# Key tiles summed in float32 while the activations are made, in a two-block transformer kernel

## The chip, the cores and the metric

One Trainium2 chip, one of its cores. The metric is device time in microseconds for one execution of the whole program, as the median of several runs; smaller is better.

## What is computed

Two transformer blocks on 256 tokens of width 2048, in float32. The part that matters is the passage from the first layer to the second: the layer norm of layer 0 ends, its result is scaled and shifted by the modulation of the condition vector, and keys, values and a forget gate are projected from it.

```python
def shared_kv(x, c_act, w_mod_kv, b_mod_kv, w_kv, b_f):
    mod = c_act @ w_mod_kv + b_mod_kv
    shift, scale = jnp.split(mod, 2, axis=-1)
    hk = x * (1.0 + scale[:, None]) + shift[:, None]
    kvf = hk @ w_kv
    k, v, zf = jnp.split(kvf, [B_WIDTH, 2 * B_WIDTH], axis=-1)
    ...
```

Here `hk` is 256 x 2048 and `w_kv` is 2048 x 4112: 16 column tiles of 128 for the keys, as many for the values, and 16 columns for the gate. Ahead of it stands layer 0 (differential attention, output projection, layer norm), behind it forgetting attention with its query/gate projection and output projection, then a second block: a state-space mixer (S5) with a gated output (GLU) and an MLP.

## The kernel before

Activations lie transposed: 16 tiles (index kt, or j where they are made) of 128 channels by 256 tokens.

**Projections.** A float32 product is made of three matmuls on reduced-precision float32 (fp32r): the weights are split into a high part `wh` and a remainder `wl`, the activations likewise into `aH` and `aL`. `mm_t` (L153) sums one column tile: for each of 16 kt, `wh` with `aH` (L163), `wh` with `aL` (L164), `wl` with `aH` (L165), 48 matmuls. `mm_n` (L188) does the same for the values with activations and weights exchanged. The weights of one column tile are 1 MB, loaded as two halves on SP's queue into four `raw` buffers and split by ScalarE (`wh`, L134) and VectorE (`wl`, L135) into five buffers of each kind. `prefetch` (L140) does this two column tiles ahead.

**Background work.** `weights()` (L144) is called once for each column tile. Apart from the prefetch it issues one step of background work (`bg`, L293) and one or more steps of a side job (`step`, L273). The background work is the modulation sums, matrix-vector products in 224 steps over the whole program, named m0, mk, m1, mc, m12, m2 and so on: each step loads two blocks of 512 KB (`graw`, four buffers, L268) and adds them up on TensorE (L222) or on VectorE into `gacc` (L237), as a cyclic list for each stage says ("policy"; the sums of mc run on TensorE always). Eight steps make a half, which TensorE closes (L246, L252). The order of the jobs is fixed, so a step not issued in one stage is issued in the next. A step's sum is issued one call behind its load. `bg_finish` issues what is left of a job where its result is needed.

**Side jobs.** In the key/value stage the side job is `s5_outputs_table` (L599), a generator that is resumed 33 times and makes a table for the later S5 mixer in 16 blocks: VectorE products (`vprod`, L554 and L555) and their sums (L635, L637), ScalarE copies (L644 to L646), small matmuls `kps` (L649) and stores. In the query/gate stage and the output projection of layer 1 it is `ctx_states` (L1279), which starts when mc is closed and is resumed 42 times: an opening with `sf` (L1296), then eight blocks of five steps each, with matmuls `inc` (L697) and on VectorE a tree of products and sums (L1337 to L1340) that ends in a copy (L1343). What is left of a side job at the end of its stage is issued by `flush`.

**Order.** The program is written in one order and a scheduler, which simulates the engines, puts the instructions of each engine's queue in the order in which they run; what is earlier in the program has priority among what is ready. `issue_after(x)` puts the instructions of its block that are on x's engine behind x; those on other engines are not bound.

**The passage.** `layer1` (L1118) makes the activations `k_` in `affine_split` (L412): for each j, `norm` adds and multiplies on VectorE (L1112, L1113), ScalarE makes `u` (L417) and its high part (L419), VectorE the remainder `kL` (L420). Six background steps follow (`BG_K`, L1126). Then come 16 key tiles by `mm_t` and 16 calls of `mm_n` for the values, the gate's sums `zf` (L1143 to L1145) behind the first key tile, and ScalarE copies of the results (L1183, L1192), each followed for the keys by a scaling of the residual in place (L1184). Next stages: the affine of the second normed input, query/gate tiles, output projection with norm, S5.

**A similar piece further on.** The GLU opens the sums of four column pairs while its own activations are still being made, in float32 with unsplit weights (`open_sums`, L1453 to L1461), in the same PSUM pool `pj` (four banks) that the projections use.

The small tiles `u` come from a pool of six buffers that other short-lived tiles share.

Of the kernel before, what the change touches and what calls it, by code (L numbers as in the profile page):

```python
# [3 lines left out]

# [7 lines left out]
F32 = mybir.dt.float32  # L12
F32R = mybir.dt.float32r
I32 = mybir.dt.int32
AF = mybir.ActivationFunctionType
# [6 lines left out]
T = 256  # L22
KT = 16
# [23 lines left out]

KO_J = 4
KO_K = 8
P_START = ("pe",)  # L50
P_L0A = ('dve', 'pe')
P_KV = ('dve', 'pe')
# [15 lines left out]
BG_K = 6  # L68
# [13 lines left out]
E_K = "x"  # L82
# [24 lines left out]
class K:  # L107
# [164 lines left out]

    def step(self):  # L273

        while self.side and next(self.side[0], True):
            self.side.pop(0)

    def flush(self, job):
        while job in self.side:
# [422 lines left out]
    def run(self):  # L702
        tc, I = self.tc, self.I
        from contextlib import ExitStack
        with ExitStack() as es:
            pool = lambda name, bufs, **kw: es.enter_context(tc.tile_pool(name=name, bufs=bufs, **kw))
            dp = pool("scratch", 1, space=DRAM)
            self.d_w = dp.tile([16, 128, 1024], F32, name="d_w")
            self.d_v = dp.tile([8, 128, 16, 128], F32, name="d_v")
            self.d_m = dp.tile([16, 128, 256], F32, name="d_m")  # L710
            self.d_l = dp.tile([128, 16, 128], F32, name="d_l")
            self.d_pw = dp.tile([128, 6, 512], F32, name="d_pw")
            self.d_b = dp.tile([16, 128, 256], F32, name="d_b")
            self.cp = pool("consts", 1)
            self.vt = pool("vecs", 1)
            self.sm = pool("small", 6)
            self.raw = pool("raw", 4)
            self.rg = pool("rg", 4)
            self.t1 = pool("t1", 6)
            self.ga = pool("ga", 1)  # L720
            self.sq = pool("sq", 2)
            self.pj = pool("pj", NPJ, space=PSUM)
            self.m = pool("m", 8 - NPJ, space=PSUM)
            xr = pool("xres", 1)
            self.hl = pool("hl", HL)
            self.bgq = []
            self.late = []
            self.hold = HOLD
            self.steps = itertools.cycle((1,))
            self.open = False  # L730
            self.side = []
            self.x = xr.tile([128, KT, T], F32, name="xres")
            mod = lambda n: self.vt.tile([128, KT], F32, name=n)
            self.m0 = [mod(f"m0_{i}") for i in range(3)]
            self.m1 = [mod(f"m1_{i}") for i in range(3)]
            self.mk = [mod(f"mk_{i}") for i in range(2)]
            self.m2 = [mod(f"m2_{i}") for i in range(6)]
            self.mc = [mod(f"mc_{i}") for i in range(2)]
            w0, w1, wk, w2 = I["w_mod0"], I["w_mod1"], I["w_kvmod"], I["w_mod2"]
            g0 = lambda i: (f"m0_{i}", self.gemv(w0, 6144, i, "c", [self.m0[i]], [f"bm0_{i}"]))  # L740
            g1 = lambda i: (f"m1_{i}", self.gemv(w1, 6144, i, "c", [self.m1[i]], [f"bm1_{i}"]))
            g2 = lambda i: (f"m2_{i}", self.gemv(w2, 12288, i, "c2", [self.m2[i]], [f"bm2_{i}"]))
            gk = lambda i: (f"mk_{i}", self.gemv(wk, 4096, i, "c", [self.mk[i]], [f"bkv_{i}"]))
            gc = lambda i: (f"mc_{i}", self.gemv(w2, 12288, i, "c2", [self.m2[i], self.mc[i]],
                                                 [f"bm2_{i}", f"bm2_{i}"]))
            jobs = {"m0": (g0(1), g0(0)), "m02": (g0(2),), "mc": (gc(1), gc(0)), "mk": (gk(1), gk(0)),
                    "m1": (g1(1), g1(0)), "m12": (g1(2),), "m22": (g2(2),), "m24": (g2(4), g2(3)), "m25": (g2(5),)}
            for n in JOBS:
                self.bg_add(*jobs[n])
            items = [I["a_v"][j - 32] if 32 <= j < 48 else I["a_in"][j] for j in self.a_order()]  # L750
            items += [I["a_out"][j] for j in range(16)]
            items += [I["kv_k"][j] for j in range(16)] + [I["kv_v"][j] for j in range(16)]
            items += [I["b_in"][h + 16 * i] for h in range(16) for i in range(2)]
            items += [I["b_out"][j] for j in range(16)]
            items += [I["glu"][j + 16 * i] for j in range(16) for i in range(2)]
            for q in range(4):
                items += [I["mlp_in"][q * 16 + j] for j in range(16)]
                items += [I["mlp_out"][q, j] for j in range(16)]
            self.stream_init(items)
            g0 = items.index(next(x for x in items if x.tensor is I["glu"].tensor))  # L760
            self.second_only = set(range(g0, g0 + 2 * KO_J))
            self.limit = 160

            with tc.tile_pool(name="act", bufs=5) as self.act:
                self.startup()
                self.layer0()
            with tc.tile_pool(name="kv", bufs=32) as self.kv, tc.tile_pool(name="act1", bufs=3) as self.act:
                self.layer1()
            with tc.tile_pool(name="s5u", bufs=1) as self.up:
                with tc.tile_pool(name="s5s", bufs=1) as self.sp:  # L770
                    self.s5_mix()
                with tc.tile_pool(name="act3", bufs=4) as self.act:
                    h_ = self.mlp_inputs()
                    self.mlp(h_)
# [90 lines left out]
    def startup(self):  # L865
        nc, I = self.nc, self.I
        self.s5_load()
        self.consts()
        self.policy(P_START, X_START)
        self.bg(12)  # L870
# [245 lines left out]
        return (norm, rb) if rms else norm  # L1116

    def layer1(self):  # L1118
        nc, V = self.nc, self.V
        z = self.x  # L1120
        for n in ("mk_1", "mk_0"):
            self.bg_finish(n)
        S, B = self.small_bg("lk", V("lg0"), self.mk[1], V("lb0"), self.mk[0])
        k_ = self.pair("k")
        self.affine_split(self.norm, S, B, k_)
        self.bg(BG_K, E_K)  # L1126
        Fs = self.cp.tile([48, T], F32R, name="Fs")
        nid = self.cp.tile([48, 16], F32R, name="nid")
        FT = self.cp.tile([128, 2, 16], F32, name="FT")
# [41 lines left out]
        kT, v = [], []  # L1171
        self.policy(P_KV, X_KV)
        vgen = self.s5_outputs_table(self.act.tile([128, 4096], F32, name="gen2_ws", tag="act"))
        self.side.append(vgen)
        for j in range(32):
            if j == 1:
                F = forget()
            if j == 3:
                forget_t(F)
            if j < 16:  # L1180
                ps = self.mm_t(k_)
                t = self.kv.tile([128, T], F32, name=f"k{j}", tag="kv")
                with self.tc.issue_after(nc.scalar.copy(t, ps).ins):  # L1183
                    nc.scalar.activation(z[:, j], z[:, j], AF.Identity, scale=V("lg0")[:, j:j + 1],  # L1184
                                         bias=V("lb0")[:, j:j + 1])
                kT.append(t)
            else:
                ps = self.mm_n(k_, j % 2)
                if j % 2:
                    for h in range(2):  # L1190
                        t = self.kv.tile([128, 2, 128], F32, name=f"v{j - 17 + h}", tag="kv")
                        nc.scalar.copy(t, ps[:, :, h * 128:h * 128 + 128])  # L1192
                        v.append(t)
        self.flush(vgen)
        for i in (1, 0):
            self.bg_finish(f"m1_{i}")
        s1 = self.plus1("s1_1", self.m1[1])
# [7 lines left out]
        a = ws[:, 512:896]  # L1205
        aT = ws[:, 896:1280]
        o = []
# [49 lines left out]
        for h in range(16):  # L1257
            start_ctx()
            ps = self.mm_t(h_)
# [3 lines left out]
            ps = self.mm_t(h_)  # L1263
# [82 lines left out]
    def s5_mix(self):  # L1346
# [118 lines left out]
        for n, b in enumerate(blocks):  # L1465
# [49 lines left out]
            for s in range(2):  # L1515
# [8 lines left out]
                if n in POOL_V:  # L1524
                    zh = self.tmp("zh")
                    nc.scalar.mul(zh, ztf, 0.5)
                    nc.gpsimd.tensor_sub(aL, zh, aH)
                    if 2 * b + s < KO_K:
                        late.append((2 * b + s, zh))
# [27 lines left out]
        for j in range(KT):  # L1557
            if j < KO_J:
                pa, pg = [self.mm_t(z_, kts[KO_K:], ko[j][:, i], i == 1) for i in range(2)]
            else:  # L1560
# [105 lines left out]
def _cols(w):  # L1666

    k, n = w.shape
    return np.ascontiguousarray(w.reshape(k // 128, 128, n // 128, 128).transpose(2, 1, 0, 3)).reshape(
        n // 128, 128, k)  # L1670


def _cols2(w):

    k, n = w.shape
    return np.ascontiguousarray(w.reshape(2, 8, 128, n // 256, 256).transpose(3, 0, 2, 1, 4)).reshape(
        n // 128, 128, k)
# [10 lines left out]
def _layout(i):  # L1688
    a = {n: np.asarray(v) for n, v in i.items() if not n.startswith("hg_")}
    o = {}  # L1690
# [13 lines left out]
    for n, ix in VEC.items():  # L1704
# [14 lines left out]
    o["a_v"] = _cols2(a["a_w_in"][0][:, 4096:6144])  # L1719
    o["a_out"] = _cols(a["a_w_out"][0])  # L1720
    o["kv_k"] = _cols(a["kv_w"][:, :2048])
    o["kv_v"] = _cols2(a["kv_w"][:, 2048:4096])
    o["wz"] = a["kv_w"][:, 4096:].reshape(KT, 128, 16).transpose(1, 0, 2)
    o["b_in"] = _cols(a["b_w_in"][0])
# [2 lines left out]

    o["glu0"] = a["s5_w_glu_2"][0][:128 * KO_K].reshape(KO_K, 128, 2, 16, 128)[:, :, :, :KO_J].transpose(
        0, 1, 3, 2, 4).reshape(KO_K, 128, 256 * KO_J)
    o["mlp_in"] = _cols(a["w_mlp_in_2"][0])  # L1730
# [33 lines left out]
```

## Time and profile before

| what | us |
|---|---|
| median of 3 runs | 2543.52 (2540.8 to 2544.13) |
| profiled execution, own time | 2548.22 |
| its span, first to last instruction | 2546.4 |

| engine | busy us | share of the span |
|---|---|---|
| TensorE (PE) | 2377.1 | 93% |
| its weight loads (PEld) | 2051.9 | 81% |
| VectorE (DVE) | 1776.8 | 70% |
| ScalarE (ACT) | 1239.5 | 49% |
| GpSimd (POOL) | 118.8 | 5% |

The mean clock granted to TensorE is 0.964 of full speed. The profile is of one execution. Busy shares are means over stages with different limits, so they are read by stage: the key/value activations are made from 696 to 736 us of the span, and the key/value projections follow up to about 963. A matmul's duration in the profile overlaps with the next one's, so the cost of one in a dense row is the distance between starts.

### The profile page before, as it was taken

The numbers are of one execution on the slowest core, as the hardware profiler recorded it, in microseconds if no ns is written. First come the engines' busy times: TensorE is split into PE (matmuls) and PEld (weight loads), VectorE is DVE, ScalarE is ACT, GpSimd is POOL, SyncE is SP. The second block draws the span as 40 slices with busy tenths as digits, with TensorE's granted clock in tenths as the row PEclk, the third lists the DMA queues.
The fourth block names the chain that finished last, engine by engine and source line by source line (L and its number), as shares of the span: only waits on it lengthen the run. The fifth ranks groups of instructions, "written<-read, shape, count | busy, mean of one in ns | idle before, by whom it ended". The sixth has DMA issues, their size and how long they took to land.

```text
span 2546.4 us, 47968 instructions
## 1 busy us (share of the span) xinstructions
PE 2377.1 (93%) x18854; PEld 2051.9 (81%) x18854; DVE 1776.8 (70%) x3360; ACT 1239.5 (49%) x2153; POOL 118.8 (5%) x234
## 2 busy tenths in 40 slices
PE   5699999999899999999998874999899999999997
PEld 1299999999678888988886663898688888888885
DVE  3288778877775555778788997877854565665655
ACT  0554554444365556666653543544544443443442
POOL 0000000000002110000000021000000000000000
PEclk9999999999889999999998886999899999999998
DMA  9999999878769998878786762998366666666652
GB/s 325 339 344 325 323 321 344 306 275 316 265 226 342 327 332 290 296 248 290 257 273 230 233 210 77 334 320 279 118 186 187 186 187 191 189 190 184 189 182 91
DMA packets 203316, 644.66 MB, mean 253 GB/s; under 512 B 41009, under 2 KB 49457, under 8 KB 202705
## 3 DMA queue, kind: packets, MB, share of 16 engines
q1 hardware_dynamic: 195616, 620.47, 72.7%
q0 software_dynamic: 7472, 21.11, 2.1%
q8 instruction: 148, 2.42, 0.4%
q14 instruction: 80, 0.65, 0.1%
HBM read 613.71 MB, written 25.69 MB: 251 GB/s over the span
## 4 chain that ended last, share of the span: by engine, by line
PE 84%; DVE 9%; DMA 3%; ACT 2%; issue 1%; SPq 0%; POOL 0%; DVEq 0%; ACTq 0%; POOLq 0%
PE pj L176 18%; PE pj L163 12%; PE pj L164 12%; PE pj L165 12%; PE pj L177 9%; PE g L222 3%; PE pjv L200 3%; DMA graw<-in_w_mod 3%; PE pjv L201 2%; PE pjv L202 2%; DVE scan_t L1415 2%; DVE scan_t L1417 2%; DVE S L1419 2%; PE inc L697 2%; PE st L370 1%
## 5 line engine op out<-in xcount | busy, mean ns | idle before, releaser
L135 DVE TENSOR_TENSOR wl<-w,wh 128x1024 fp32r<-128x1024 f32 x631 | 770.0, 1224 | 465.2 <-ACT wh L134 457.2
L134 ACT CAST wh<-w 128x1024 fp32r<-128x1024 f32 x632 | 659.1, 1050 | 711.1 <-PE pj L176 283.0
L176 PE MATMUL pj<-h,wh 128*128 128x512 f32 x1024 | 362.9, 399 | 6.8 <-DVE h L420 5.0
L176 PE MATMUL pj<-d,wh 128*128 128x512 f32 x1024 | 360.3, 398 | 0.0
L237 DVE SCALAR_TENSOR_TENSOR gacc<-graw,csilu,gacc 128x1024 f32<-128x1024 f32 x211 | 270.2, 1281 | 27.4 <-DMA graw<-in_w_mod 18.6
L177 PE MATMUL pj<-h,wl 128*128 128x256 f32 x1024 | 287.5, 281 | 1.1 <-DVE wl L135 1.1
L177 PE MATMUL pj<-d,wl 128*128 128x256 f32 x1024 | 285.8, 280 | 0.0
L176 PEld LDWEIGHTS pj<-h,wh 128*128 128x128 f32 x1024 | 193.1, 189 | 55.8 <-issue 4.0
L176 PEld LDWEIGHTS pj<-d,wh 128*128 128x128 f32 x1024 | 192.0, 188 | 48.2 <-PE pj L177 1.7
L163 PE MATMUL pj<-hH,wh 128*128 128x256 f32 x768 | 221.6, 289 | 6.2 <-ACT hH L419 4.0
L165 PE MATMUL pj<-hH,wl 128*128 128x256 f32 x768 | 221.4, 289 | 0.5 <-DVE wl L135 0.5
L164 PE MATMUL pj<-hL,wh 128*128 128x256 f32 x768 | 221.1, 288 | 0.0
L222 PE MATMUL g<-graw,czc 128*32 128x256 f32 x1744 | 168.4, 469 | 49.6 <-DMA graw<-in_w_mod 48.0
L177 PEld LDWEIGHTS pj<-h,wl 128*128 128x128 f32 x1024 | 194.0, 189 | 1.5 <-DVE wl L135 1.5
L177 PEld LDWEIGHTS pj<-d,wl 128*128 128x128 f32 x1024 | 193.1, 189 | 0.4
L163 PEld LDWEIGHTS pj<-hH,wh 128*128 128x128 f32 x768 | 148.8, 194 | 9.8 <-ACT hH L419 4.1
L165 PEld LDWEIGHTS pj<-hH,wl 128*128 128x128 f32 x768 | 148.6, 194 | 4.5 <-issue 3.3
L164 PEld LDWEIGHTS pj<-hL,wh 128*128 128x128 f32 x768 | 148.9, 194 | 3.8 <-issue 3.7
L222 PEld LDWEIGHTS g<-graw,czc 128*32 128x32 f32 x1744 | 46.0, 119 | 129.4 <-DMA graw<-in_w_mod 105.5
L163 PE MATMUL pj<-h1H,wh 128*128 128x256 f32 x512 | 147.1, 290 | 0.3 <-ACT ctx_ws L1323 0.2
L164 PE MATMUL pj<-h1L,wh 128*128 128x256 f32 x512 | 146.4, 287 | 0.0
L165 PE MATMUL pj<-h1H,wl 128*128 128x256 f32 x512 | 146.0, 286 | 0.0
(480 smaller groups left out, 5201.4 us busy)
## 6 DMA issues: line engine op xcount, KB each, us to landing
graw<-in_w_mod SPq DMA_DIRECT2D x384, 512.0 KB, 5.8
w<-in_mlp_in SPq DMA_DIRECT2D x128, 512.0 KB, 4.3
w<-in_mlp_out SPq DMA_DIRECT2D x128, 512.0 KB, 4.3
w<-in_a_in SPq DMA_DIRECT2D x96, 512.0 KB, 6.3
graw<-in_w_kvmod SPq DMA_DIRECT2D x64, 512.0 KB, 6.6
w<-in_b_in SPq DMA_DIRECT2D x64, 512.0 KB, 5.8
w<-in_glu SPq DMA_DIRECT2D x56, 512.0 KB, 5.3
w<-in_a_v SPq DMA_DIRECT2D x32, 512.0 KB, 5.9
```

Of the source, the lines that this page charges most:

```text
L134: nc.scalar.copy(h, src)
L135: (eng or (nc.gpsimd if next(self.spl) else nc.vector)).tensor_sub(l, src, h)
L163: self.nc.tensor.matmul(ps, h, aH, start=kt == order[0] and not opened, stop=False)
L164: self.nc.tensor.matmul(ps, h, aL, start=False, stop=False)
L165: self.nc.tensor.matmul(ps, l, aH, start=False, stop=kt == order[-1] and last)
L176: self.nc.tensor.matmul(ps, h, view(aH, 0, [[T, 2], [1, T]]), start=kt == order[0], stop=False)
L177: self.nc.tensor.matmul(ps[:, 0], l, aH, start=False, stop=kt == order[-1])
L200: self.nc.tensor.matmul(ps[:, i], aH[:, s], h, start=half == 0 and i == 0 and k == 0, stop=False)
L201: self.nc.tensor.matmul(ps[:, i], aH[:, s], l, start=False, stop=False)
L202: self.nc.tensor.matmul(ps[:, i], aL[:, s], h, start=False, stop=half == 1 and i == 1 and k == 7)
L222: nc.tensor.matmul(st["g"][32 * q:32 * q + 32], self.cz[c][:, ch * 2 + s], raw[s][:, q * 256:q * 256 + 256], start=st["n"] == 0, stop=ch = ...
L237: nc.vector.scalar_tensor_tensor(acc, raw[s], cc, acc, op0=MUL, op1=ADD)
```

## The change

The first four key tiles (`KH = 4`) no longer go through `mm_t`. Their weights come unsplit, in eight loads that each hold two kt of all four tiles, from an input laid out for it (`kv0`), into the `raw` buffers. As soon as `u` of a kt is made, four float32 matmuls add its product to four sums, which lie in two PSUM banks. The high part and the remainder of the activations are still made, for the other tiles. The list of split weights begins with the fifth key tile. The six background steps are bound behind the last `kL`, as far as they are on VectorE. So is the table job's VectorE work; that job starts with tile 4 (`LATE_V`) and is resumed once, once, once and twice in turn (`P_VT`). The gate's sums move from behind tile 0 to behind tile 4, and `forget_t` likewise.

```diff
+KH = 4
+LATE_V = 4
+P_VT = (1, 1, 1, 2)
...
     def step(self):
-        while self.side and next(self.side[0], True):
-            self.side.pop(0)
+        with self.tc.issue_after(self.after) if self.after else nullcontext():
+            while self.side and next(self.side[0], True):
+                self.side.pop(0)
...
-            items += [I["kv_k"][j] for j in range(16)] + [I["kv_v"][j] for j in range(16)]
+            items += [I["kv_k"][j] for j in range(KH, 16)] + [I["kv_v"][j] for j in range(16)]
...
         k_ = self.pair("k")
-        self.affine_split(self.norm, S, B, k_)
-        self.bg(BG_K, E_K)
+        head = [self.pj.tile([128, 2, T], F32, name="kh", tag="pj") for _ in range(KH // 2)]
+        for j in range(KT):
+            if j % 2 == 0:
+                w = self.raw.tile([128, 2, KH, 128], F32, name="wkh", tag="raw")
+                nc.sync.dma_start(w.rearrange("p a j c -> p (a j c)"), I["kv0"][j // 2])
+            u = self.tmp("u")
+            nc.scalar.activation(u, self.norm(j), AF.Identity, scale=S[:, j:j + 1], bias=B[:, j:j + 1])
+            for i in range(KH):
+                nc.tensor.matmul(head[i // 2][:, i % 2], w[:, j % 2, i], u, start=j == 0 and i % 2 == 0,
+                                 stop=j == KT - 1 and i % 2 == 1)
+            aH, aL = k_(j)
+            nc.scalar.copy(aH, u)
+            last = nc.vector.tensor_sub(aL, u, aH).ins
+        with self.tc.issue_after(last):
+            self.bg(BG_K, E_K)
+        self.after = last
...
-        self.side.append(vgen)
         for j in range(32):
-            if j == 1:
+            if j == LATE_V:
+                self.side.append(vgen)
+                self.steps = itertools.cycle(P_VT)
+            if j == KH + 1:
                 F = forget()
-            if j == 3:
+            if j == KH + 3:
                 forget_t(F)
             if j < 16:
-                ps = self.mm_t(k_)
+                ps = head[j // 2][:, j % 2] if j < KH else self.mm_t(k_)
...
         self.flush(vgen)
+        self.steps = itertools.cycle((1,))
+        self.after = None
...
+    o["kv0"] = a["kv_w"][:, :128 * KH].reshape(8, 2, 128, 128 * KH).transpose(0, 2, 1, 3).reshape(8, 128, 256 * KH)
```

## Rows read from the trace of the kernel before

**Rows 1.** Windows: engine busy us (instructions), TensorE's clock, DMA share, GB/s.
```profile
696.00:736.00 40.00, 31.17 (x166) 28.59 (x167) 37.15 (x74) 21.58 (x44) 2.00 (x5) 0.68 0.64 200
736.00:962.00 226.00, 226.00 (x2361) 196.61 (x2361) 132.89 (x186) 126.67 (x239) 38.61 (x84) 1.00 0.94 323
```
**Rows 2.** Groups on VectorE, 696 to 733 us: count | busy us, mean ns | idle before.
```profile
L237 DVE SCALAR_TENSOR_TENSOR gacc<-graw,csilu,gacc 128x1024 f32<-128x1024 f32 x7 | 9.0, 1284 | 0.0
...
L135 DVE TENSOR_TENSOR wl<-w,wh 128x1024 fp32r<-128x1024 f32 x4 | 4.9, 1232 | 0.0
...
L554 DVE TENSOR_TENSOR vprod<-gen_ws 128x512 f32<-128x512 f32 x4 | 2.8, 694 | 0.0
```
**Rows 3.** Timeline of VectorE in the same stage: start us, us, instruction.
```profile
707.83 1.28 DVE L237 SCALAR_TENSOR_TENSOR gacc<-graw,csilu,gacc 128x1024 f32<-128x1024 f32 x1
709.03 0.42 DVE L1113 TENSOR_TENSOR xres<-xres,lnb 128x256 f32<-128x256 f32 x1
709.36 0.42 DVE L1112 TENSOR_TENSOR xres<-xres,lnb 128x256 f32<-128x256 f32 x1
```
**Rows 4.** Timeline of TensorE, the first key tiles and the gate's first matmul.
```profile
698.09 1.01 PE L163 MATMUL pj<-kH,wh 128*128 128x256 f32 x3 [2.10 <-ACT kH L419]
...
700.08 0.41 PE L164 MATMUL pj<-kL,wh 128*128 128x256 f32 x1
700.29 0.41 PE L165 MATMUL pj<-kH,wl 128*128 128x256 f32 x1
...
704.67 0.28 PE L165 MATMUL pj<-kH,wl 128*128 128x256 f32 x1
704.79 0.28 PE L164 MATMUL pj<-kL,wh 128*128 128x256 f32 x1
...
736.06 0.28 PE L1143 MATMUL zf<-kH,wzH 128*16 128x256 f32 x1
```
**Rows 5.** Groups on TensorE, 697.6 to 736 us.
```profile
L164 PE MATMUL pj<-kL,wh 128*128 128x256 f32 x54 | 19.8, 374 | 4.8 <-DVE kL L420 4.8
L165 PE MATMUL pj<-kH,wl 128*128 128x256 f32 x53 | 18.5, 354 | 1.2 <-DVE wl L135 1.2
L163 PE MATMUL pj<-kH,wh 128*128 128x256 f32 x55 | 15.7, 359 | 2.9 <-ACT kH L419 2.9
```
**Rows 6.** Timeline of TensorE, open sums of the GLU in float32.
```profile
1498.83 8.86 PE L1461 MATMUL ko<-zh,wko 128*128 128x256 f32 x32 [2.53 <-ACT zh L1526]
...
1509.34 7.17 PE L1461 MATMUL ko<-zh,wko 128*128 128x256 f32 x32
```
**Rows 7.** Timeline of ScalarE, the first activation of the key/value input.
```profile
697.00 0.60 ACT L417 ACTIVATE u<-xres,lkb,lks 128x256 f32<-128x256 f32 x1 [2.10 <-DVE xres L1113]
```
**Rows 8.** Timeline of SP's queue, a weight load ahead of the stage.
```profile
685.47 0.33 SPq L130 DMA_DIRECT2D w<-in_kv_k  x1
```
**Rows 9.** Timeline of TensorE, the table job's last matmuls.
```profile
978.29 0.59 PE L649 MATMUL kps<-gen_ws 128*32 128x112 f32 x16
```
**Rows 10.** Chain of work, one background step on TensorE: start us, us.
```profile
743.72 1.00 PE g L222 x16
```
**Rows 11.** One line's instructions, the opening of the context job.
```profile
L1296 PE MATMUL sf<-ctx_ws,esel x32: 209/209/230, 1036.4 to 1037.3; 128*64 128x16 f32 x32
```
**Rows 12.** Chain of work, the first inc of the context job's last block.
```profile
1347.41 1.89 PE inc L697 x30
```
**Rows 13.** One line's instructions, the copies that end the context job's blocks.
```profile
L1343 DVE COPY s<-ctx_ws x8: 186/194/195, 1093.5 to 1378.5; 128x32 f32<-128x32 f32 x8
```
**Rows 14.** Groups on VectorE, 1349 to 1379 us: the tree's large operations.
```profile
L1337 DVE TENSOR_TENSOR ctx_ws<-ctx_ws 128x512 f32<-128x512 f32 x3 | 2.1, 693 | 2.6 <-ACT ctx_ws L1323 2.6
```
**Rows 15.** Windows at the start of S5, columns as in rows 1.
```profile
1372.00:1382.00 10.00, 6.83 (x58) 4.54 (x58) 7.76 (x38) 2.83 (x8) 0.00 (x0) 0.92 1.02 410
1382.00:1392.00 10.00, 5.28 (x27) 3.39 (x25) 9.57 (x31) 5.37 (x14) 1.31 (x3) 0.50 0.42 150
```
**Rows 16.** One line's instructions, gacc between 1373 and 1392 us.
```profile
L237 DVE SCALAR_TENSOR_TENSOR gacc<-graw,csilu,gacc x3: 1277/1278/1280, 1375.4 to 1384.1; 128x1024 f32<-128x1024 f32 x3
```

More of the change, by code (lines that the diff above doesn't have):

```diff
@@ L1 @@
 import functools
+from contextlib import nullcontext
 import itertools
@@ L1118, in layer1 @@
     def layer1(self):
-        nc, V = self.nc, self.V
+        nc, V, I = self.nc, self.V, self.I
         z = self.x
@@ L1194, in layer1 @@
         self.flush(vgen)
+        self.steps = itertools.cycle((1,))
+        self.after = None
         for i in (1, 0):
```

## The prediction

> **What bounds the kernel now.** I read the table of windows first. From 736 to 962 us TensorE is busy for all of 226 us at full clock, with DMA at 0.94 of its time; from 696 to 736, where the key/value activations are made, it is busy for 31 of 40 us at a mean clock of 0.68, and VectorE is busy for 37 [rows 1]. So the stage before 736 belongs to VectorE, the one behind it to TensorE, and what counts is how much of TensorE's work is done when the first ends.
>
> The groups of VectorE say with what it fills those 37 us [rows 2]. Its own work there is three operations for each of 16 column tiles (add, multiply, kL), issued 0.33 us apart [rows 3]: 16 x 3 x 0.33 = 16 us. The rest is not needed there: 7 gacc at a pitch of 1.20 [rows 3] make 8.4, 4 weight remainders wl at 1.14 (1.23 less the overlap that gacc shows) 4.6, and 12 operations of the table (vprod, and the sums that read it) at up to 0.69 make 8.3. Together 37. TensorE waits: its rows of L163 to L165 have 4.8 us of waits for kL and 2.9 for kH, and it drops to half clock (a pitch of 0.21 instead of 0.12) [rows 4, 5].
>
> **Part 1: the head.** Four key tiles leave the split path. Removed: 4 x 48 matmuls at 0.12 = 23.0 us, and eight casts and eight wl. Added: 16 x 4 = 64 float32 matmuls with unsplit weights. The same kind stands in the trace: the GLU's open sums, 128x256 float32, where one matmul shows as two records and 32 records take 7.17 us at full clock [rows 6]. That is 0.448 us a matmul, 28.7 us for 64: TensorE gets 5.7 us more to do. It pays because of where it is done. For a tile, VectorE now needs 1.0 us and TensorE 1.79, so TensorE no longer starves, and the clock should come back and stay.
>
> The Trainium skill (FP8 and Floating Point Precision, TensorE Precision Notes) states four passes through the array for true float32, where the split needs three. By it the 64 cost 256 x 0.12 = 30.7 us instead of 28.7, and the sum would be 2.0 us worse.
>
> Start: the first u ends at 697.60 [rows 7]. Half clock at the start: the first 32 records of the open sums lost 8.86 - 7.17 = 1.7 us [rows 6]; in the present stage the pitch is 0.12 again only at about 704.4, 6.3 us behind the first matmul at 698.09, half of which, 3.2, would be lost [rows 4]. I take 2.5. End of the head: 697.6 + 28.7 + 2.5 = 728.8.
>
> Before, zf begins at 736.06 [rows 4], with 55 + 54 + 53 = 162 matmuls of key tiles done [rows 5]: three tiles and 18 of the fourth. The 30 missing take 3.6 us, so four tiles of work are done at 739.7. **Gain 10.9 us.**
>
> Its cover, piece by piece. The eight weight loads (512 KB each) share the raw buffers with the split weights; before, such loads were issued up to 685.5 [rows 8], so the first ones wait for TensorE at 697.6. Each later load has two tiles' time, 3.6 us, and four buffers. On SP they stand ahead of the loads of gacc that must wait for buffers, since those are freed only behind the last kL. If that order is reversed, one landing of about 6 us is added. The u tiles share six buffers, and TensorE now releases them: u of tile 15 needs tile 9 done (about 718), so ScalarE is held at TensorE's pace, with the casts of later weights queued behind it, and the last kL comes at about 720. The tiles behind the head (columns 4 and 5) were split during the output projection, so nothing is waiting at 729. The 16 us of gacc, table and so on go behind the last kL, where VectorE is busy for 133 of 226 us [rows 1]: free, for the casts and remainders of four tiles are gone from it. The table runs at five steps for four tiles, 35 steps over 28 calls where 33 are needed, and ends about two calls ahead of the stage's end. Before, its last kps runs at 978 [rows 9], inside the next affine stage, as filling for TensorE. It moves into the dense part and costs about 1.6 us there, and the ScalarE copies that fed it leave an affine stage that is busy on ScalarE. I set this at 0, between -2 and +2.
>
> **Part 2: four calls fewer.** Each weights() call also issues one step of the modulation sums and one of a side job. Counted through the policies, the key/value stage has 28 instead of 32 steps; all four missing are TensorE steps of mc. 16 records of L222 take 1.00 us [rows 10], so **-4.0 us**. The missing ones run in the query/gate stage, where mc closes behind call 10 instead of 6: 17 TensorE steps instead of 14, **+3.0 us**. At the far end five gacc steps move to the last GLU calls and three (six gacc of 1.28 us) into the MLP's start, where VectorE makes activations: 0 if gaps take them, 5 if most lie on the path. I take **+2**.
>
> **Part 3: the context states.** They start when mc is closed, four calls later (call 12; before at call 8, sf at 1036 [rows 11]). They take 41 steps at one a call: before, 24 + 16 calls and a remainder; now 20 + 16, so the whole last block falls behind the output norm. From the query/gate stage two groups of inc (1.9 each [rows 12]) leave: **-3.8 us**. Behind the norm VectorE gets the tree of that block. The four large operations of L1337 to L1340 stand three times each, 2.1 us a line [rows 14]: 8.4 busy, 7.2 at a pitch of 0.60, and about 3.3 for the smaller levels, 10.5 in all. There VectorE has 2.2 us idle in 1372 to 1382 and next to none in 1382 to 1392 [rows 15]. In exchange the open half of m2 (three gacc, 1375 to 1384, 3.6 us at their pitch [rows 16]) is gone, since in the new order no half is open at that point. 10.5 - 2.2 - 2.3 (a share of those gacc) = **+6**, between 0 (all fits in the waits of the norm's chain) and 10.5.
>
> **Sum:** -10.9 - 4.0 + 3.0 + 2 - 3.8 + 6 = -7.7 us. Against the profiled execution's 2548.2 that is 2540.5; that execution lies 4.7 above the median of the runs, so against 2543.5 it is 2535.8.
>
> **Rivals.**
> 1. *The later stages give nothing back* (both + terms at 0): -15.7, 2527.8. For: the norm's chain is short operations with latencies between. Against: VectorE is full from 1382 on.
> 2. *It is taken back on the way, no change.* Two ways. The key/value stage moves 226 x 323 = 73 MB; with held loads of gacc and of the table added (about 5.6 MB), four steps and two earlier loaded tiles gone (6.3 MB), some 72.3 MB must pass in about 211 us, 343 GB/s, and if 323 were the most this mix allows, the stage would take 224, +13 us, at most the whole gain. Against: 323 came at a share of 0.94, and TensorE had no idle time [rows 1]. Or the hold on VectorE doesn't work and a tile goes on taking 37/16 = 2.3 us; then the head ends at about 735 and 6 us are lost: -1.5, 2542.
> 3. *The context block holds the S5 stage: slower.* Place: the first norms of S5, in the window from 1382 [rows 15]. If the last block runs only behind the last projection matmul (an estimate of 1373, inside the window from 1372) and takes the 31 us that it took before (from its first inc at 1347 to the last copy of L1343 at 1378.5 [rows 12, 13]), it ends at 1404, and if the norms stand behind its tree on VectorE, S5 starts 21 us late instead of 6: +7.6, 2551. It decides from a delay of about 14 us. Against: much of those 31 us is waiting between calls.
> 4. *The head stays at half clock: slower still.* 64 x 0.448 x 2 = 57.3 us, end 755 instead of 728.8: +18.5, 2562. For: the clock fell again in this stage when TensorE had gaps. Against: the head leaves it none, and the open sums got full clock [rows 6].
>
> **Numbers.** Forecast 0.62, rival 1 0.18, rival 2 0.10, rival 3 0.07, rival 4 0.03. A measurement of this kernel tells about 0.2%, 5 us, from no change. Four fifths of the forecast's own spread (2530 to 2541, by the terms' bounds) lie beyond that: faster 0.62 x 0.8 + 0.18 = 0.68; within 0.2%: 0.12 + 0.10 = 0.22; slower 0.10. The range takes in rivals 1 and 2, 2526 to 2546; left out are rivals 3 and 4 and the outer ends of the terms.
>
> **What would show it.** Right: kh matmuls begin at about 697.6 and end at 727 to 731 with no wait inside, clock full from about 703; gacc and vprod only behind the last kL at about 720; the first key/value split tile's matmuls directly behind; the key/value stage's last copy some 15 us earlier; the first norm of S5 some 9 us earlier than before, not 15. Wrong: waits of kh matmuls for wkh, a head beyond 735, TensorE idle for weights in the key/value stage, or the start of S5 later than before.

## The result and the profile after

**Slower.** The changed kernel takes 2567.07 us (median of 4 runs, 2563.57 to 2571.32), the kernel before, run beside it, 2542.82 (2540.8 to 2544.13): ratio 1.0097, 95% interval 1.0085 to 1.011. That is 24 us more, where 8 us less was forecast and the range ended at 2546. The profiled execution after took 2571.32 us, with a span of 2569.5; it lies 4.3 above its median, and that of before 4.7 above the median shown with it, so the two traces can be set side by side as they are.

The head itself did what was forecast. In the changed kernel, one line's instructions (count: shortest/median/longest ns, first and last start) and the windows around it (busy us of each engine, clock, DMA share, GB/s):

```profile
L1141 PE MATMUL kh<-u,wkh x128: 377/379/792, 694.0 to 725.1; 128*128 128x256 f32 x128
```
```profile
692.00:700.00 8.00, 6.34 (x21) 5.15 (x20) 7.43 (x21) 6.52 (x17) 0.00 (x0) 0.57 0.00 0
700.00:727.00 27.00, 27.00 (x135) 24.00 (x134) 20.36 (x41) 12.69 (x27) 0.47 (x1) 1.00 0.60 195
```

128 records from 694.0 to 725.1, full clock from 700 on. The sums stand at 725, not at 739.7. And yet the last two columns already show what went wrong: DMA stood still up to 700 and then ran at 0.60.

Three lines on the way (the last one is the end of the table job). Before, as far as it was not shown:

```profile
L1192 ACT COPY v<-pjv x16: 363/374/378, 855.6 to 963.3; 128x256 f32<-128x256 f32 x16
...
L1260 ACT ACTIVATE ws<-pj x16: 364/378/386, 987.8 to 1234.1; 128x256 f32<-128x256 f32 x16
...
L649 PE MATMUL kps<-gen_ws x512: 259/259/284, 736.4 to 978.6; 128*32 128x112 f32 x171
```

After:

```profile
L1216 ACT COPY v<-pjv x16: 352/373/379, 828.0 to 940.8; 128x256 f32<-128x256 f32 x16
...
L1286 ACT ACTIVATE ws<-pj x16: 372/378/384, 976.5 to 1227.8; 128x256 f32<-128x256 f32 x16
...
L655 PE MATMUL kps<-gen_ws x512: 256/259/283, 759.4 to 997.2; 128*32 128x112 f32 x171
```

The last value copy comes 22.5 us earlier, the first query result only 11.3, the last one 6.3, and the table, which was to end two calls ahead of the stage's end, ends 56 us behind the last value copy and 19 later than before. From the start of S5 on the changed kernel is behind: the first evacuation of S is at 1406.8 instead of 1399.7, the last at 1462.4 instead of 1444.6, the first product of the MLP at 1850.5 instead of 1824.2. So some 20 us were gained up to the value copies, and 45 were lost behind them.

**Where the loads are.** The DMA issues between 655 and 717 us (count, KB each, median us to landing), before and then after:

```profile
graw<-in_w_mod SPq DMA_DIRECT2D x19, 512.0 KB, 4.8
w<-in_kv_k SPq DMA_DIRECT2D x8, 512.0 KB, 5.2
```
```profile
wkh<-in_kv SPq DMA_DIRECT2D x8, 512.0 KB, 3.4
w<-in_kv_k SPq DMA_DIRECT2D x5, 512.0 KB, 4.2
graw<-in_w_mod SPq DMA_DIRECT2D x1, 512.0 KB, 4.6
```

Nineteen loads of the modulation sums before, one after. Their buffers come free when gacc has used them, and VectorE's timeline of the changed kernel has no gacc between these two:

```profile
655.86 1.28 DVE L242 SCALAR_TENSOR_TENSOR gacc<-graw,csilu,gacc 128x1024 f32<-128x1024 f32 x1
716.52 1.28 DVE L242 SCALAR_TENSOR_TENSOR gacc<-graw,csilu,gacc 128x1024 f32<-128x1024 f32 x1
```

Before, that stretch held 17 of them, nine between 657 and 688, ahead of the first norm, where VectorE has room for them. In windows from 660 to 730 and from 730 to 940, before:

```profile
660.00:730.00 70.00, 56.66 (x320) 44.84 (x320) 58.25 (x104) 31.59 (x59) 3.03 (x11) 0.76 0.73 234
730.00:940.00 210.00, 210.00 (x2185) 182.72 (x2183) 122.32 (x171) 116.47 (x222) 35.20 (x76) 1.00 0.92 320
```

and after:

```profile
660.00:730.00 70.00, 65.51 (x383) 53.81 (x382) 43.38 (x92) 33.34 (x68) 1.93 (x9) 0.95 0.48 151
730.00:940.00 210.00, 207.12 (x2041) 180.40 (x2044) 129.25 (x168) 109.58 (x200) 31.51 (x64) 0.99 0.92 326
```

(234 - 151) GB/s x 70 us = 5.8 MB less were moved ahead of 730; at the 326 GB/s of the stage behind, they take 17.8 us there.

**S5.** SP's queue at its start, before and after (start us, us in the queue):

```profile
1374.70 11.03 SPq L268 DMA_DIRECT2D graw<-in_w_mod  x5
1394.05 2.13 SPq L684 DMA_DIRECT2D U<-ub  x2
...
1440.18 1.37 SPq L268 DMA_DIRECT2D graw<-in_w_mod  x3
```
```profile
1372.08 30.61 SPq L273 DMA_DIRECT2D graw<-in_w_mod  x10
1402.74 1.30 SPq L690 DMA_DIRECT2D U<-ub  x2
1404.14 0.79 SPq L273 DMA_DIRECT2D graw<-in_w_mod  x1
...
1409.94 2.81 SPq L273 DMA_DIRECT2D graw<-in_w_mod  x4
...
1421.71 1.53 SPq L273 DMA_DIRECT2D graw<-in_w_mod  x3
```

Before, five loads of sums, and the next ones when the state matmuls were done (1440). After, ten loads ahead of the first write of U and eight more between the blocks. On TensorE it is the same: before, the first state matmuls (`inc`, 1396.41) precede the next matmuls of sums on loaded blocks (from 1438.72); after, 72 records of sums stand ahead of the first `inc` at 1403.97.

**The MLP's start.** VectorE's groups from the last GLU product to the first product of the MLP, after:

```profile
L242 DVE SCALAR_TENSOR_TENSOR gacc<-graw,csilu,gacc 128x1024 f32<-128x1024 f32 x12 | 15.3, 1278 | 0.0
L140 DVE TENSOR_TENSOR wl<-w,wh 128x1024 fp32r<-128x1024 f32 x8 | 9.8, 1219 | 3.8 <-ACT wh L139 3.8
```

Before, there is no gacc in that stretch. It takes 57.0 us (1793.5 to 1850.5) instead of 44.7 (1779.5 to 1824.2).

### The profile page after: what moved, and what is told of

Read it like the earlier page. It is cut to its first block, busy times and chain, and to the rows that moved or that the text cites. A ratio compares the mean times of both kernels' runs of the same rounds, so it can differ in the third digit from the quotient of the medians.

```text
span 2569.5 us, 47772 instructions
## 1 busy us (share of the span) xinstructions
PE 2374.4 (92%) x18774; PEld 2043.7 (80%) x18774; DVE 1772.2 (69%) x3355; ACT 1231.8 (48%) x2145; POOL 119.9 (5%) x233
## 4 chain that ended last, share of the span: by engine, by line
PE 83%; DVE 9%; DMA 5%; ACT 2%; issue 1%; SPq 0%; POOL 0%; DVEq 0%; ACTq 0%; POOLq 0%
PE pj L181 18%; PE pj L168 11%; PE pj L170 11%; PE pj L169 11%; PE pj L182 9%; DMA graw<-in_w_mod 4%; PE g L227 3%; PE pjv L206 2%; PE pjv L205 2%; PE pjv L207 2%; DVE scan_t L1441 2%; DVE scan_t L1443 2%; DVE S L1445 2%; PE inc L703 2%; PE kh L1141 1%
## 5 line engine op out<-in xcount | busy, mean ns | idle before, releaser
L140 DVE TENSOR_TENSOR wl<-w,wh 128x1024 fp32r<-128x1024 f32 x624 | 761.3, 1222 | 460.6 <-ACT wh L139 450.5
L139 ACT CAST wh<-w 128x1024 fp32r<-128x1024 f32 x624 | 650.0, 1049 | 718.1 <-PE pj L181 281.2
L181 PE MATMUL pj<-h,wh 128*128 128x512 f32 x1024 | 365.2, 401 | 10.9 <-DVE h L426 9.1
```

What stands on the lines that cost most here:

```text
L139: nc.scalar.copy(h, src)
L140: (eng or (nc.gpsimd if next(self.spl) else nc.vector)).tensor_sub(l, src, h)
L181: self.nc.tensor.matmul(ps, h, view(aH, 0, [[T, 2], [1, T]]), start=kt == order[0], stop=False)
```

## The experiments

The theories: **L**, the loss is the sums running four steps late; **T**, it is the late table; **D**, which came from the first four runs, the stage goes at the pace of DMA and loads were taken out of the head. All results are medians in us; "before" is the kernel before on the same chip, 2543.92 in the first four runs, 2543.65 in the next, 2543.39 in the last. Each of these kernels ran four times, two of them more. The moments (a copy, a first result) are read from one profiled execution of each kernel, which lies between 4.9 us under the median (run 9) and 4.7 over it (run 5 and the kernel before), so a few us between two traces prove nothing by themselves.

**1. The sums' four steps back (e1).** In the loop over the keys:

```diff
+            if j < KH:
+                self.bg()
```

> The changed kernel with one addition: each of the four keys of the head again issues one step of the modulation sums, so that every later stage finds the sums where they stood before the change. Theory L (the loss is the sums running four steps late): the key/value stage gets its 4 us back, the query/gate stage, the start of S5, the S5 stage up to the last evacuation and the start of the MLP lose the 5, 11, 11 and 7 us that they had gained in length; in all about 2567 + 4 - 34 = 2537 us, and the loads of the sums in S5 stand behind the W stage again (last evacuation of S about 1440 us). Theory T (what costs is the table job, which now ends 56 us behind the last value copy): no more than 5 us better, 2562 or above.

2563.55, ratio 1.0078 (1.0059 to 1.0097): only 3.5 better than the change. Theory L alone falls here. In S5 the loads are behind the state matmuls again, as expected, but the time is lost earlier: the first query result comes at 996.5, 8.7 later than before, though the last value copy is at 934.5.

**2. The lag alone (e2).** The kernel before, in which the first four key tiles issue no step of the sums (`skip` is set to 4 at the start of the stage).

```diff
-        self.bg()
+        if self.skip:
+            self.skip -= 1
+        else:
+            self.bg()
```

> The kernel before, with no change but this: the first four key tiles issue no step of the sums; the tiles, the table and the calls stay as they were. Theory L: the key/value stage is 4 us shorter, and then S5's start, S5 and the MLP's start lose about 29 us: 2543 - 4 + 29 = 2568 us, with no float32 head in it. Theory T, or a fault of the head itself: 2539 to 2543 us, the sums being late costs nothing.

2572.1, ratio 1.0115 (1.0098 to 1.0132): 28 slower, as theory L said, without any float32 head. Up to the last query result it is 2.4 us ahead; then it has the ten loads ahead of U (from 1375.27, 30.89 us in the queue), the first GLU product 15.2 late, and in front of the MLP:

```profile
L240 DVE SCALAR_TENSOR_TENSOR gacc<-graw,csilu,gacc 128x1024 f32<-128x1024 f32 x12 | 15.4, 1282 | 0.0
```

So late sums are dear by themselves, and yet putting them back into the changed kernel did not help. Both hold if the changed kernel's key/value stage has no room for them.

**3. S5's sums behind its state matmuls (e3).**

```diff
-                    nc.sync.dma_start(w.rearrange("p i r x -> p (i r x)"), self.d_w[2 * b + q])
+                    wl_last = nc.sync.dma_start(w.rearrange("p i r x -> p (i r x)"), self.d_w[2 * b + q]).ins
...
-        self.bg(BG_M)
+        with self.tc.issue_after(wl_last):
+            self.bg(BG_M)
```

> The changed kernel, in which the loads of the twelve steps of sums of the S5 stage are bound behind the last load of wl; the sums stay four steps late. If it is the place of these sums in the S5 stage that costs (their matmuls ahead of and between the state matmuls, their loads ahead of U and wl on SP): the stage from the first to the last evacuation of S is 45 us instead of 56 and its start some 4 us earlier, 2567 - 15 = 2552 us. If the stage is long because the tree of the context states ends late: no change, 2565 to 2569.

2558.55, ratio 1.0066 (1.0049 to 1.0083): 8.5 better, of the 15 expected. The first evacuation of S is at 1399.3 instead of 1406.8, the last at 1451.0 instead of 1462.4, so the stage is 52 us instead of 56, not 45. The place of the sums is a part of the price in S5, not all of it. The MLP's start keeps its price: 55.6 us.

**4. Only the head left (e4).** The sums' and the table's four steps back, the table not held:

```diff
-        self.after = last
...
-            if j == LATE_V:
+            if j == 0:
                 self.side.append(vgen)
-                self.steps = itertools.cycle(P_VT)
+            if j < KH:
+                self.bg()
+                self.step()
```

> The changed kernel in which only the head is left of the change: the four keys of the head issue a step of the sums and one of the table each, one step a call, and the table is not held behind the last kL. Theory L alone: the same as the kernel with the sums back, 2537. If the late table costs too (the first query tile came 11 us later after the last value copy than before): another 5 to 10 us better, 2528 to 2532, the first query result about 5 us nearer to the last value copy. If the hold was needed: the head ends at 735 instead of 727 and the gain is gone, 2540 or above.

2554.99, ratio 1.0048 (1.0032 to 1.0065): still 11 slower than before. The last record of the float32 sums starts at 722.3, the last value copy is at 935.8, 27.5 ahead of before; the first query result is at 986.4, 1.4 ahead. Its windows say where it went:

```profile
660.00:730.00 70.00, 65.50 (x387) 54.42 (x387) 44.98 (x96) 33.65 (x68) 3.02 (x11) 0.95 0.51 165
730.00:940.00 210.00, 206.35 (x2060) 177.92 (x2059) 130.75 (x168) 107.37 (x195) 31.45 (x66) 1.00 0.92 327
930.00:970.00 40.00, 23.67 (x258) 13.45 (x251) 17.76 (x34) 18.73 (x46) 8.77 (x20) 0.66 0.93 325
```

From 930 to 970 TensorE is busy for 24 of 40 us, while DMA is at 0.93 of its time, and TensorE's waits name `graw` from DMA first (10.0 us, 7 times). The loads are the limit, and ahead of 730 only 165 GB/s were moved. This gave theory D.

**5. The hold taken off the sums (e5).** As 4, and:

```diff
-        with self.tc.issue_after(last):
-            self.bg(BG_K, E_K)
+        self.bg(BG_K, E_K)
```

> The kernel with only the head left (sums and table steps back, table not held), and in addition the six steps of sums behind the head are no longer held behind the last kL, so that their buffers come free and their loads go on while the head runs. Theory D (the key/value stage and the passage into the query/gate stage go at the pace of DMA; in 660 to 730 us the head kernel moved 10 to 11 MB where the kernel before moved 16, and what is not loaded there has to be loaded later at some 325 GB/s): up to 5 MB earlier, 8 to 15 us, 2540 to 2547. Rival H (VectorE must be kept free in the head): the head ends some us later than 722 and the time is 2555 or above.

**2532.46, ratio 0.9959 (0.9943 to 0.9975)**: 22.5 better than 4, more than expected, and 11.2 faster than before. Nineteen loads of sums lie between 655 and 717 again:

```profile
660.00:730.00 70.00, 63.55 (x383) 51.16 (x383) 56.01 (x103) 27.60 (x54) 2.47 (x10) 0.93 0.80 257
730.00:940.00 210.00, 206.84 (x2157) 178.27 (x2155) 122.21 (x174) 116.73 (x226) 40.06 (x82) 1.00 0.94 327
```

The head does get longer, as rival H said (run 10 shows with what): its last record starts at 737.1 instead of 722.3, and the last value copy is at 956.7 instead of 935.8. Yet the first query result is at 974.0, 12.4 earlier than in 4 and 13.8 earlier than before, and most of that lasts: the last query result is 12.6 ahead of before, the end 11.2.

**6 and 7. Half of the sums' loads left out in the key/value stage**, in kernel 4 (e6) and in the kernel before (e7): the second block of a step isn't loaded, the first is used for both (`half` is set for this stage alone).

```diff
                 for i in range(2):
+                    if i and self.half:
+                        raw.append(raw[0])
+                        continue
                     raw.append(self.rg.tile([128, 1024], F32, name="graw", tag="graw"))
```

> The kernel with only the head left, but each step of sums issued in the key/value stage loads one of its two blocks and uses it for both (the second half of the rows of the sums is left out there; instructions of the engines are the same), 16 MB less to load. Theory D: the stage is TensorE's again, the first query result comes 15 to 20 us earlier than 986, the whole about 2537. If DMA does not limit this stage: 986 and 2553 to 2556 as with all loads.

> The same loads left out in the kernel before. Theory D: there TensorE had no idle time in this stage, so nothing is to be had: last value copy 960 to 964, 2540 to 2545. If the loads limit the stage before too: earlier by 10 us or more.

In kernel 4: 2529.54, ratio 0.9943 (0.9927 to 0.996), 25 better than with all loads, with the hold still in place; the first query result is at 967.7, 18.7 earlier, and TensorE has no idle time from 930 to 970:

```profile
930.00:970.00 40.00, 40.00 (x382) 34.99 (x374) 19.12 (x34) 29.36 (x60) 4.70 (x12) 1.00 0.77 261
```

In the kernel before the same edit brings nothing: 2553.02, ratio 1.0041 (1.0027 to 1.0056), 9 slower. So the loads don't limit this stage in the kernel before. With the hold they do, here behind the head, and by run 12 it seems without the head too. Run 6 leaves out far more than the hold had displaced, and it relieves DMA, the turn in SP's queue and the four `graw` buffers at once; which of the three sets the pace isn't separated, and "the pace of DMA" stands for all of them. That fewer loads make the kernel before slower was not expected by either theory: TensorE is busy for 203 of 210 us there, with a wait of 4.28 us for a ScalarE copy of the sums, in an order that the scheduler chose anew. It was not followed further.

**8. Sixteen steps instead of twelve in S5, gated as in 3 (e8).** `BG_M = 16`.

> The changed kernel with the sums of S5 bound behind the last load of wl, as in the gated run, and sixteen instead of twelve of them there, so that the GLU and the MLP find the sums where they stood before the change. Theory L: the 11 us that the gated run lost from the scan's end to the end of the program against the kernel before come back, 2547 to 2550. If the GLU and MLP are late for another reason: 2557 to 2560.

2556.73, ratio 1.005 (1.0035 to 1.0065): 1.8 better than 3, not 11. The MLP's start takes 49.0 us instead of 55.6, with four gacc instead of twelve. But the sixteen steps are in the way of the S5 outputs: the GLU's open sums begin at 1511.0 instead of 1501.9, behind a wait of 5.38 us for the table `vl`. So four steps issued late were paid for at each place that was tried.

**9. The hold off, and nothing else undone (e9).** The edit of 5 in the changed kernel.

> The changed kernel with one thing undone: the six steps of sums behind the head are not held behind the last kL. Theory D plus L (the hold costs some 22 us of DMA time, and the sums being four steps late costs 28 to 30 by itself): the key/value stage is no longer short of loads, the loss by the lag stays; 2532 + 28 = about 2558 us, between 2552 and 2562. Theory D alone (the hold is the whole fault): 2567 - 22 = 2545 us or below.

2559.8, ratio 1.0073 (1.0056 to 1.009). As D plus L said: the first query result at 964.5 is the earliest of all, and S5 and the MLP (12 gacc at its start, 15.4 us) then lose it. The hold was not the whole fault.

**10. As 5, the table alone held (e10).**

```diff
         self.bg(BG_K, E_K)
+        self.after = last
```

> The kernel with head, sums and table steps back and the sums not held, in which only the table's VectorE work is held behind the last kL. If VectorE is what stretches the head to 38 us there (8 us of table work in it): the head ends at about 729 and the time is 2526 to 2530. If the table then runs late into the query/gate stage: no gain, 2532 to 2540.

2531.15, ratio 0.9957 (0.9942 to 0.9972). The head ends at 729.4, as expected, but the time is 1 above the range that went with it, and it is that of 5 within the spread. What TensorE did for the split tiles (`pj`) between the head's first and last matmul says why, in 5 and then here (us, busy and count, clock, DMA share, GB/s):

```profile
699.10:737.30 38.20, 12.30 (x65) 0.93 0.81 260
696.40:729.60 33.20, 5.47 (x25) 0.92 0.78 258
```

The 8 us by which the head of 5 ends later were not lost: 2.7 are its later start, and in most of the rest TensorE did matmuls of the next tiles between those of the head, 65 instead of 25, which at 0.12 us each is 4.8 us. From 660 to 730 it is busy for 63.55 us in both; here:

```profile
660.00:730.00 70.00, 63.55 (x364) 51.00 (x363) 56.47 (x105) 32.53 (x65) 2.48 (x10) 0.93 0.77 252
```

So the table's work on VectorE stretched the head, but TensorE didn't wait for it. The hold on the table costs nothing here.

**11. As 5, the six steps of sums on TensorE (e11).**

```diff
-        self.bg(BG_K, E_K)
+        self.bg(BG_K, "pe")
```

> The same kernel with nothing held, in which the six steps of sums behind the head run on TensorE instead of VectorE. Their loads need no place on VectorE to come free; TensorE gets some 6 us, VectorE loses some 14. Theory D: the loads are as early as with VectorE, the head is shorter than 38 us, 2527 to 2533. If what counts is VectorE's share alone, and TensorE is full: 2534 to 2540.

2544.45, ratio 1.0007 (0.9998 to 1.0017). A miss, slower than either range. The head is short (last record at 724.7), but only ten loads of sums lie between 655 and 717, 216 GB/s from 660 to 730, and the table ends at 994.9. On VectorE those sums filled the wait ahead of the norm; on TensorE they did so only in part. The 41 GB/s that are missing against 5 make 2.9 MB in 70 us, by an estimate at 326 GB/s 9 us. But the first query result is at 975.5, only 1.5 behind 5; it is 12.3 ahead of before, and at the last query result 5.1 of that are left. How much each has to do with the 12 us was not separated.

**12. The hold alone, in the kernel before (e12).** `affine_split` returns its last kL, and:

```diff
-        self.affine_split(self.norm, S, B, k_)
-        self.bg(BG_K, E_K)
+        last = self.affine_split(self.norm, S, B, k_)
+        with self.tc.issue_after(last):
+            self.bg(BG_K, E_K)
```

> The kernel before with the hold alone: the six steps of sums bound behind the last kL, no float32 head, no late sums. Theory D: 12 loads of 512 KB go from the idle DMA time in 655 to 730 into the full stage behind it, against some 7 us less VectorE work in the stage of the activations: 5 to 12 us slower, 2549 to 2556. If VectorE's share of that stage is what counts: 5 to 7 us faster, 2536 to 2539.

2557.12, ratio 1.0058 (1.0043 to 1.0074): 13.7 slower, as D said. It repeats the changed kernel's picture without a float32 head: one load of sums between 655 and 717, the last value copy at 937.7, 25.6 earlier than before, and the first query result at 1000.0, 12.2 later.

```profile
660.00:730.00 70.00, 60.29 (x414) 50.16 (x413) 49.10 (x99) 37.22 (x71) 3.02 (x11) 0.93 0.42 138
```

**Put together**, in us against the kernel before:

| | no head | head, sums not held | head, sums held |
|---|---|---|---|
| sums on time | 0 | -11.2 (5), -12.2 (10) | +11.1 (4), +19.6 (1) |
| sums four steps late | +28.2 (2) | +16.4 (9) | +24.3 (the change) |

The head is worth -11, the hold +22 with the sums on time (and +13.7 with no head, run 12), the lag +28 (0 to 28.2, and -11.2 to 16.4). In 1, 9 and the change the table is late and held too; between 4 and 1, where nothing else differs, that costs 8.5. The prices don't add up fully: -11 + 22 + 28 would be +39, the change is +24, and with the sums held the lag costs only 4.7 (against 1, by that edit alone) to 13 (against 4). Where the stage is short of loads, four steps fewer are 4.2 MB fewer, by an estimate 13 us at 326 GB/s, which is about what is missing; no run tests it.

## Why the prediction was wrong

**Part 1, the head: right in itself.** Forecast were kh matmuls with no wait inside, full clock from about 703, and 31.2 us from the first to the last. Measured: no wait inside (one of 1.7 us for u lies ahead of the first), full clock from 700, 694.0 to 725.1, begun 3.6 us earlier than forecast. With the sums left where they were it is worth 11.2 (5) and 12.2 (10), where 10.9 was forecast. By the forecast's own reckoning, the moment when four tiles' work is done, which was 739.7 before, run 5 gains 739.7 + 65 x 0.12 - 737.5 = 10.0 and run 10 739.7 + 25 x 0.12 - 729.8 = 12.9. So the mechanism held; the end of the head alone, 2.2 and 9.9, doesn't show it.

**The step that failed first: its cover.** "The 16 us of gacc, table and so on go behind the last kL, where VectorE is busy for 133 of 226 us [rows 1]: free". Two things were wrong with it. It counted the seven gacc that [rows 2] show from 696 on, but the hold binds the whole of the six steps and, as their order is fixed, what follows them; nine of the gacc had run before 688, in a stretch that the prediction never looked at. And it priced what is held by VectorE's time only. A gacc also frees the buffer into which the next load goes, so what is held is loads: 18 of 19 in 62 us. The prediction did see that loads move ("held loads of gacc and of the table added (about 5.6 MB)"; measured 5.8), but put them into rival 2 alone, which got 0.10, and there against it that the stage had 0.94 and TensorE no idle time [rows 1]. That TensorE has no idle time tells that DMA was not yet the limit, not that it has room: 0.94 leaves 14 us in 226, and the edit took work from TensorE and added loads. Rival 2 put the price at up to 13; the hold alone measured 13.7, and behind the head 22.

**The same shortage reaches the table.** "Ends about two calls ahead of the stage's end" was counted in calls. Its loads stand in SP's queue among those of the weights and sums, and in run 4 its products waited 10.1 us for them between 926 and 1010. The last kps came at 997.2 with a pace of five steps for four tiles, at 998.8 with one step a tile (run 4), at 972.0 when the sums' loads lay in the head again (run 5). The affine term, set at 0, is a part of this: the passage from the last value copy to the first query result took 35.7 us instead of 24.5.

**The step that failed worst: parts 2 and 3, four steps late.** The sum there was -4.0 + 3.0 + 2 - 3.8 + 6 = +3.2. Run 2 has the lag without the head: +28.2. By its terms:

- Key/value and query/gate stage, -4.0 + 3.0 - 3.8 = -4.8: the right side, and about half of it. Run 2 is 2.4 ahead at the last query result.
- S5's start, "+6, between 0 and 10.5": the tree did come into the norm's chain. It stands between every two of its small operations, and TensorE waits 7.7 us for rc instead of 2.2. The first evacuation of S came 7.1 late in the change, after a query/gate stage that ended 6.3 early: 13.4 instead of 6 (11.1 in run 2). What is missing in the term is the open half: "the open half of m2 ... is gone" was booked as a gain of 2.3. With it the following twelve steps, which had stood behind the state matmuls, moved to the front, on SP's queue, on DMA (a share of 1.01 from 1400 to 1430) and on TensorE. Binding them gave 8.5 back (run 3). That the open half was what had kept them back is read from the order only; the binding was tried, the half was not.
- MLP's start, "+2, 0 if gaps take them, 5 if most lie on the path": measured 12.3 (57.0 - 44.7). Twelve gacc of 1.28 us, not six, and gaps take little of their 15.3 us; with four of them (run 8) it is 4.3.

**Rival 3** named the right side and a part of the place: S5 late, because of the context block. Its delay, 13.4 us here and 10.8 in run 3, where the sums are out of the way, came near its point of 14 without reaching it. The rest of the loss came from the sums inside S5 and further on, which the rival did not have. **Rival 1**, that nothing is given back, failed most. **Rival 4** failed: the clock came back, as [rows 6] had shown for the open sums.

**A marker that misled.** "The key/value stage's last copy some 15 us earlier" was named as a sign that the forecast is right. It came 22.5 earlier here, 25.6 in run 12, which is slower than before. What was not loaded in time (sums, table) went behind that copy, so it measures the order and not the progress. The first query result is better, but it doesn't need the table or the sums of mc: it moved by -11.3 here, -13.8 in 5 and -1.4 in 4, but by -12.3 in 11, which is no faster than before. In the runs with the sums on time and the table's end behind that result (1, 4, 11, 12), 3 to 8 us more are lost by the last query result; with the table's end ahead of it (5, 6, 7, 10) it is 1 us or none. The last query result agrees with the end of the same trace to 6 us in all eight of these. That is a pattern of the traces; it was not tested.

## What to carry to other kernels

Before background work is held back to free an engine, look at what its buffers let in: here the held consumer kept back the loads behind it, and a stage that ran at 0.92 of DMA's time could not take 5.8 MB more without loss. Work that is issued one step per call is a clock for the whole program; when calls go, put the steps back where they were, and look at each place where the missing ones will land. Judge a stage by a result that needs everything issued in it, side jobs and sums too; neither the end of the head, nor the last copy, nor the first query result was one here. Let the edits be tried one by one: the head was worth 11 us, and two side edits made for it or by it turned that into a loss of 24.

## What the runs showed of the hardware

DMA's pace in the stage was not one number: 369 GB/s from 730 to 770 in the changed kernel, 389 in run 1, where nearly all are 512 KB loads that had been waiting, and 320 to 336 GB/s over 730 to 940 in the kernels that loaded everything, at shares of 0.91 to 0.96 (run 2, whose first four steps fall away there, 305 at 0.87). The Trainium skill (DMA: Bandwidth & Descriptors, Specifications) lists about 358 GB/s from HBM for one core, as half of what a stack gives to two. This program runs on one core; its 389 GB/s over 40 us, with DMA at 1.00 of its time, is above that, and the longer stretches with the table's stores are below it.

A float32 matmul of 128 x 256 cost less than in [rows 6]: 112 records in 24.33 us, 0.217 us a record or 0.43 a matmul, at full clock. An estimate from the Trainium skill's four passes for true float32 (FP8 and Floating Point Precision, TensorE Precision Notes), each at the 0.12 us of a matmul of the split, is 0.48 us. The trace is a tenth below it; whether there are fewer passes, or each is shorter than a matmul of the split, no run here shows.

```profile
701.10 24.33 PE L1141 MATMUL kh<-u,wkh 128*128 128x256 f32 x112
```
